# A decoder layer on one core: which engine splits the memory's weights, where the S5 output is split, who takes the heads' roots, and how the first norm is finished

## The chip, the core and the metric

The kernel runs on one core of a Trainium2 chip. The core has a matrix engine (TensorE, PE in the rows; its weight loads are shown as PEld), a vector engine (VectorE, DVE), a scalar engine (ScalarE, ACT), a general engine (POOL, GpSimd) and a queue for transfers (SyncE, SP). Each engine works through its own list in order; semaphores tie the lists together. The metric is the device time of one execution in microseconds, the median of several.

## The reference

One decoder layer in float32 for 1024 tokens of width 1024, with a memory of 256 tokens. Cut to what the change touches:

```
h = layer_norm(x); mem_n = layer_norm(mem)
z = h @ w_in                                   # S5 input | q k | v | r | low-rank gate
y_ssm = gelu-GLU of a diagonal state-space scan over 32 groups
o = chunked gated linear attention, 4 heads of 128 values
o = o * rsqrt(mean(o*o, -1) + 1e-5) * norm_g * silu(r)     # one root per token and head
y = concat(y_ssm, o) @ w_out
h = layer_norm(2**0.25 * h + y)                # the first norm of the layer
kv = mem_n @ w_mkv; p = softmax(q k^T / 16); h = layer_norm(2**0.25 * h + (p v) @ w_mo)
h = layer_norm(2**0.25 * h + relu(h @ w_ff1)**2 @ w_ff2)
```

## The kernel before

**Splits.** Products that need float32 accuracy are made of three products of rounded parts: `split` lets ScalarE write the rounded high part and VectorE or POOL subtract it from the source for the low part; `mm3` runs high x high, high x low, low x high. A weight block of 128 x 1024 elements (`weight`, `wcols`) is read into a `raw` buffer (four of them) through SP's queue and split into `hl`. Tables of bits (`MW`, `MW1`, `MV1` and the like) say block by block which engine subtracts: a one is VectorE, a zero POOL (`eng`). A bank of PSUM of 128 x 512 is taken by a letter: three `d`, three `s`, two `g`.

**Memory.** `mem_stream` folds the memory into two weights for each of four heads h: `a_d` (keys times w_mq) and `vw_d` (values times w_mo). For a head it transposes w_mq (`wqT`), multiplies the normed memory by the key columns (`mem_proj`, `mnT` x `hl`, result `kvT`), multiplies the two, loads the value columns, and multiplies those by w_mo. `mem_w` loads two key or two value blocks. Head 0 comes at the start of the program, heads 1 to 3 here.

**Filling.** A `Filler` holds streams of work cut into pieces of known cost and is told at fixed places in the program to run so many us of them. From the end of the S5 scan it alternates `glu_stream` (the GLU, which gates `Y0` by `y1f`, then `y_split`, which makes the parts of y that the output product reads, and the load of residual tiles `R`), and the rest of `mem_stream`; `out_stream` follows, the S5 half of the output product. Which instruction comes first on an engine is then set by a scheduler that sees the dependencies and its own costs, not by the text alone. `behind()` ties the instructions traced inside it, on VectorE alone, behind the last VectorE instruction traced before.

**Gated attention.** The chunk scores are built from seven levels. For each level and each half of the sequence (`level`), TensorE multiplies K and Q for two pairs of chunks into `g` banks (L1065), VectorE copies them by mask into `Am`, and then Q (VectorE one half of its rows, POOL the other) and K (POOL, mostly) are multiplied by the level's decay. The next level reads these. `diagonal` comes first: VectorE makes Q and the product `prod`, which lies in the tile `y1f`, and TensorE sums it against `ones2`. Then eight chunks (`gla_chunk`): update and state products, state S (POOL decays, VectorE adds), squares of the output per head by ScalarE with a sum, one root for each of 128 tokens and 4 heads (`rsqrt`, on `sq` of 128 x 4), and the scaling by ScalarE or VectorE (`ON`).

**First norm.** In the loop over `tk` the chunk `tk`, the parts of y for chunk `tk - 1` (`gla_out`) and the attention half of the output product for tile `tk - 2` (`block`, epilogue of `post_norm`) follow each other. The epilogue adds into `R`; after the second half the tile is normed by `layer_norm`, and three blocks later transposed into `h`, the operand of the next stage (L243, splits `h`). `norm_stats` takes the mean and the variance (`mv`) and a root of one column (`tq`, nine small VectorE instructions). Then, in columns:

- plain form: VectorE takes the mean off and multiplies by the gain over 1024 columns; ScalarE scales the upper 512 by the root; VectorE scales the lower 512 and adds the bias; POOL adds the bias to the upper 512;
- `light` form: VectorE does the first step on the lower 512 alone and makes the shift in one more small instruction, ScalarE norms the upper 512, and POOL multiplies and adds there, two instructions of 512 columns.

The bits of `GLN` = 53 choose light for tiles 0, 2, 4 and 5. The second norm (`ahead=True`) uses the same function and the same bits.

Of the kernel before, what the change touches and what calls it, by code (L numbers as in the profile page):

```python
# [17 lines left out]
P = 128  # L18
# [7 lines left out]
T = 8  # L26
# [18 lines left out]
MWU = 7  # L45
MQK = 3
MVV = 11
MW1 = 0
MV1 = 1
MO1 = 3  # L50
MQ0 = 255
ON = 206
# [29 lines left out]
def hybrid_layer(  # L82
# [61 lines left out]
    def stt(e, o, a, s, b, op0, op1):  # L144
        e.scalar_tensor_tensor(out=o, in0=a, scalar=s, in1=b, op0=op0, op1=op1)  # L145
# [16 lines left out]
        for n, (i, j) in enumerate(P3):  # L162
            PE.matmul(o, lhs(i), rhs(j), start=first and n == 0, stop=last and n == 2, skip_group_check=more)  # L163

    def rsqrt(e, y, v, t):
        ts(e, y.bitcast(I32), v.bitcast(I32), -0.5, 1597463007.0, ALU.mult, ALU.add)
        for _ in range(3):
            stt(e, t, y, -0.5, y, ALU.mult, ALU.mult)
            tt(e, t, t, v, ALU.mult)
            stt(e, y, t, 1.5, y, ALU.add, ALU.mult)  # L170

    def rsqrt1(y, v, eps, t):

        vh, w = t[:, 0:1], t[:, 1:2]
# [46 lines left out]
        rsqrt1(tq[:, 0:1], mv[:, 1:2], EPS, tq[:, 1:3])  # L221
        return mv, tq

    def layer_norm(xt, rows, light=False, st=None):
        mv, tq = norm_stats(xt, st)
        lo_, hi_ = slice(0, 512), slice(512, D)
        if light:
            stt(V, xt[:, lo_], xt[:, lo_], mv[:, 0:1], rows[:, 0, lo_], ALU.subtract, ALU.mult)
            stt(V, tq[:, 3:4], mv[:, 0:1], -1.0, tq[:, 0:1], ALU.mult, ALU.mult)
            act(xt[:, hi_], xt[:, hi_], AF.Identity, scale=tq[:, 0:1], bias=tq[:, 3:4])  # L230
            tt(G, xt[:, hi_], xt[:, hi_], rows[:, 0, hi_], ALU.mult)
        else:
            stt(V, xt, xt, mv[:, 0:1], rows[:, 0, :], ALU.subtract, ALU.mult)
            act(xt[:, hi_], xt[:, hi_], scale=tq[:, 0:1])
        stt(V, xt[:, lo_], xt[:, lo_], tq[:, 0:1], rows[:, 1, lo_], ALU.mult, ALU.add)
        tt(G, xt[:, hi_], xt[:, hi_], rows[:, 1, hi_], ALU.add)
# [750 lines left out]

    def y_split(th, k):
        hi, lo = (ya(0, th)[:, i, k, :].rearrange("p (c t) -> p c t", t=T) for i in range(2))
        split(hi, lo, Y0[:, k, :].rearrange("p (t c) -> p c t", t=T)[:, th * 64:(th + 1) * 64, :], scale=0.25)  # L990

    R = []

# [72 lines left out]


    prod = y1f[:, 0:2048].rearrange("p (a t) -> p a t", a=2)
    ones2 = const.tile([P, 2], F32, name="ones2")
    G.memset(ones2, 0.0)  # L1070
    for h in range(2):
        G.memset(ones2[hrow[h], h:h + 1], 1.0)

# [74 lines left out]
    def gla_chunk(tk):  # L1148
        ktm, on, sr, vt = K[:, :, tk * P:(tk + 1) * P], Am[:, tk].rearrange("p h t -> p (h t)"), sr_[tk % 2], v_[tk % 2]
        if tk < NT - 1:  # L1150
            up = bank("s", (P, 2, P))
            for a in range(2):
                for h in range(2):
                    PE.matmul(up[hrow[h], a, :], ktm[:, a, h * 64:h * 64 + 64],
                              vt[:, (2 * a + h) * P:(2 * a + h + 1) * P], start=True, stop=True)
        po = bank("g", (P, 4, P))
        for h in range(4):
            PE.matmul(po[:, h, :], Am[:, tk, h, :], vt[:, h * P:(h + 1) * P], start=True, stop=tk == 0)
            if tk:
                PE.matmul(po[:, h, :], Q[:, h // 2, h % 2, tk * P:(tk + 1) * P], S[:, h // 2, :], start=False, stop=True)  # L1160
        if tk < NT - 1:
            tt(G, S, S, dcl[:, :, tk:tk + 1].to_broadcast([P, 2, P]), ALU.mult)
            tt(V, S, S, up, ALU.add)
        if tk < NT - 2:
            gla_keys(tk + 1)
        sq = small.tile([P, 12], F32, tag="sq", name="sq")
        for h in range(4):
            act(on[:, h * P:(h + 1) * P], po[:, h, :], AF.Square, accum_out=sq[:, h:h + 1])
        ts(V, sq[:, 0:4], sq[:, 0:4], 1.0 / P, EPS, ALU.mult, ALU.add)
        rsqrt(V, sq[:, 4:8], sq[:, 0:4], sq[:, 8:12])  # L1170
        if ON >> tk & 1:
            for h in range(4):
                act(on[:, h * P:(h + 1) * P], po[:, h, :], scale=sq[:, 4 + h:5 + h])
        else:
            on4 = on.rearrange("p (h v) -> p h v", h=4)
            tt(V, on4, po, sq[:, 4:8].unsqueeze(2).to_broadcast([P, 4, P]), ALU.mult)
        tt(eng(OE, tk), on, on, sr, ALU.mult)
# [31 lines left out]
    def post_norm(put, rows, scale=ALPHA, ahead=False):  # L1209

        half = stage.tile([P, NT, 2, 6], F32, tag="cn", bufs=1, name="half") if ahead else None

        def epi(n, t, po):
            r = res(t)[:, n * 512:(n + 1) * 512]
            if scale is None:
                tt(V, r, r, po, ALU.add)
            else:
                stt(V, r, r, scale, po, ALU.mult, ALU.add)
            if n == 0:
                if ahead:  # L1220
                    V.bn_stats(out=half[:, t, 0, :], in_=r)
                late.append(lambda: None)
            else:
                layer_norm(res(t), rows, GLN >> t & 1, half[:, t] if ahead else None)
                late.append(lambda: put(t))
        return epi

# [482 lines left out]
```

## Time and profile before

| | us |
|---|---|
| median of 3 runs | 1414.79 (1411.76 to 1419.1) |
| the profiled execution | 1412.6 |
| its span | 1410.8 |
| TensorE busy | 1341.5 |
| VectorE busy | 998.0 |
| POOL busy | 460.0 |
| mean granted clock of TensorE | 0.986 |

How to read the rows: `325.10 4.63 PE L163 MATMUL ... x24 [2.22 <-DVE wqT L142]` in an order of time is the start, the length of the merged group, engine, line, operation, tile written <- tiles read, how many, and in brackets the idle time ahead of it on its engine with what ended that. L142 and L145 are the helpers `tt` and `stt`, L163 is the matmul of `mm3`, so groups are told apart by their tiles. The tile names `g` and `qk` stand for several slots: `g<-g,g` is a level's product on Q, `qk<-qk,g` that on K. Of the stages that follow: the S5 scan ends near 310, levels run from 318 to 457, chunks from 478 to 549, the first norm from 503 to 590.

### The profile page before, as it was taken

What the parts mean: (1) busy time and instruction counts of PE and PEld (TensorE: products, weight loads), DVE (VectorE), ACT (ScalarE), POOL (GpSimd) and SP (SyncE); (2) the same over time, 40 slices, a digit from 0 to 9 for tenths busy, and PEclk for the clock granted to TensorE, in tenths of its full rate; (3) what the DMA queues carried; (4) which work ended last, traced back from release to release, by engine and by line L of the source; (5) the groups of instructions that cost most, each with busy time, mean ns of one, the idle gap of its engine ahead of it and who ended that gap; (6) DMA issues with size and microseconds to landing.
All of it is one profiled execution on the core that took longest, in us unless ns stands there. A gap on an engine that the chain in (4) does not pass through costs nothing. (4 is left out here: it accounts for less than half of the span.)

```text
span 1410.8 us, 18927 instructions
## 1 busy us (share of the span) xinstructions
PE 1341.5 (95%) x6824; PEld 1112.6 (79%) x6824; DVE 998.0 (71%) x1783; ACT 570.1 (40%) x946; POOL 460.0 (33%) x338
## 2 busy tenths in 40 slices
PE   7798999999899998999998999999999999999997
PEld 6575788788898887788887777778888888888886
DVE  8999588756855489844478667766555676568797
ACT  4433532342545143333123654445545343335431
POOL 1663144312855133200014223443332142003364
PEclk9899999999999999999999999999999999999999
DMA  9722342543756120310120656554446985334432
GB/s 311 255 110 81 107 121 52 161 159 112 255 186 209 56 73 23 119 30 1 60 60 23 194 174 198 194 188 142 145 140 230 343 270 178 104 105 150 149 105 90
DMA packets 155513, 199.81 MB, mean 142 GB/s; under 512 B 16294, under 2 KB 86044, under 8 KB 155292
## 3 DMA queue, kind: packets, MB, share of 16 engines
q1 hardware_dynamic: 143536, 179.44, 39.5%
q10 hardware_dynamic: 11884, 19.17, 3.7%
q8 instruction: 54, 0.88, 0.3%
q14 instruction: 39, 0.32, 0.1%
HBM read 140.38 MB, written 58.20 MB: 141 GB/s over the span
## 5 line engine op out<-in xcount | busy, mean ns | idle before, releaser
L163 PE MATMUL ps_d<-xt,w1q 128*128 128x512 f32 x576 | 138.3, 391 | 9.8 <-DVE w1s L142 9.5
L163 PEld LDWEIGHTS ps_d<-xt,w1q 128*128 128x128 f32 x576 | 107.3, 188 | 35.4 <-issue 12.2
L142 POOL TENSOR_TENSOR hl<-raw,hl 128x1024 fp32r<-128x1024 f32 x21 | 63.0, 3006 | 168.3 <-ACT hl L148 168.2
L163 PE MATMUL ps_s<-cell 128*128 128x512 f32 x432 | 113.0, 389 | 0.0
L163 PE MATMUL ps_d<-cell 128*128 128x512 f32 x432 | 106.0, 389 | 0.4 <-DVE hid L142 0.4
L142 POOL TENSOR_TENSOR R<-R,row 128x512 f32<-128x512 f32 x42 | 57.8, 1386 | 138.4 <-ACT R L148 134.9
L163 PE MATMUL ps_d<-h0T,hl 128*128 128x512 f32 x384 | 93.6, 402 | 5.8 <-DVE hl L142 5.8
L163 PE MATMUL ps_g<-xb,w1q 128*128 128x512 f32 x384 | 94.3, 397 | 3.9 <-ACT hid L148 3.9
L163 PE MATMUL ps_d<-hl,y 128*128 128x512 f32 x384 | 95.1, 403 | 2.5 <-DVE y L142 2.5
L163 PEld LDWEIGHTS ps_d<-cell 128*128 128x128 f32 x432 | 81.0, 188 | 17.6 <-DVE hid L142 0.8
L163 PEld LDWEIGHTS ps_s<-cell 128*128 128x128 f32 x432 | 81.1, 188 | 16.8
L163 PEld LDWEIGHTS ps_d<-h0T,hl 128*128 128x128 f32 x384 | 73.2, 193 | 25.8 <-DVE hl L142 6.2
L163 PE MATMUL ps_d<-hl,h0T 128*128 128x512 f32 x384 | 91.1, 393 | 1.4 <-DVE h0T L142 1.3
L148 ACT ACTIVATE hl<-raw 128x1024 fp32r<-128x1024 f32 x62 | 64.8, 1059 | 66.1 <-PE ps_d L163 60.2
L163 PE MATMUL ps_d<-hl,p 128*128 128x512 f32 x384 | 89.0, 391 | 0.0
L163 PEld LDWEIGHTS ps_g<-xb,w1q 128*128 128x128 f32 x384 | 72.5, 191 | 19.6 <-ACT hid L148 4.7
L163 PEld LDWEIGHTS ps_d<-hl,y 128*128 128x128 f32 x384 | 72.6, 193 | 18.0 <-DVE y L142 3.0
L148 ACT ACTIVATE hid<-hid 128x512 f32<-128x512 f32 x112 | 70.8, 632 | 36.9 <-DVE hid L142 35.1
L163 PEld LDWEIGHTS ps_d<-hl,h0T 128*128 128x128 f32 x384 | 71.0, 188 | 17.3 <-DVE h0T L142 1.8
L163 PEld LDWEIGHTS ps_d<-hl,p 128*128 128x128 f32 x384 | 71.6, 188 | 14.6
L142 DVE TENSOR_TENSOR cell<-ha,cell 128x1024 fp32r<-128x1024 f32 x56 | 78.2, 1401 | 5.6 <-ACT cell L148 3.4
L148 ACT ACTIVATE w1q<-raw 128x512 fp32r<-128x512 f32 x80 | 50.0, 628 | 76.2 <-PE ps_d L163 39.6
(286 smaller groups left out, 2868.8 us busy)
## 6 DMA issues: line engine op xcount, KB each, us to landing
g_d<-hid SPq DMA_DIRECT2D x112, 256.0 KB
ha<-g_d SPq DMA_DIRECT2D x56, 512.0 KB
raw<-in_w_ff_dram SPq DMA_DIRECT2D x40, 512.0 KB
b<-in_w_ff_dram SPq DMA_DIRECT2D x32, 512.0 KB
raw<-in_w_mkv_dram SPq DMA_DIRECT2D x16, 512.0 KB
raw<-in_w_in_dram SPq DMA_DIRECT2D x16, 512.0 KB
wq<-in_w_mq_dram SPq DMA_DIRECT2D x8, 512.0 KB
xs<-in_x_dram SPq DMA_DIRECT2D x8, 512.0 KB
```

The costliest lines, as they stand in the source:

```text
L142: e.tensor_tensor(out=o, in0=a, in1=b, op=op)
L148: A.activation(out=o, in_=i, func=f, **kw)
L163: PE.matmul(o, lhs(i), rhs(j), start=first and n == 0, stop=last and n == 2, skip_group_check=more)
```

## The change

Four edits. `MW1` and `MV1` become 3: both key blocks and both value blocks of heads 1 to 3 are subtracted by VectorE (before, POOL did both key blocks and one of two value blocks; nine blocks move). `y_split` is traced inside `behind()`. In `gla_chunk` the root is no longer `rsqrt` (one instruction for the mean, one for the first guess, three rounds of three): ScalarE takes the square root of mean + 1e-5, VectorE its reciprocal and one Newton round. In the first norm no tile takes the light form any more, and tiles 5, 6 and 7 are finished by VectorE alone over 1024 columns, with neither ScalarE nor POOL.

```diff
-MW1 = 0
-MV1 = 1
+MW1 = 3
+MV1 = 3
...
-    def layer_norm(xt, rows, light=False, st=None):
+    def layer_norm(xt, rows, light=False, st=None, alone=False):
         mv, tq = norm_stats(xt, st)
         lo_, hi_ = slice(0, 512), slice(512, D)
+        if alone:
+            stt(V, xt, xt, mv[:, 0:1], rows[:, 0, :], ALU.subtract, ALU.mult)
+            stt(V, xt, xt, tq[:, 0:1], rows[:, 1, :], ALU.mult, ALU.add)
+            return
...
         hi, lo = (ya(0, th)[:, i, k, :].rearrange("p (c t) -> p c t", t=T) for i in range(2))
-        split(hi, lo, Y0[:, k, :].rearrange("p (t c) -> p c t", t=T)[:, th * 64:(th + 1) * 64, :], scale=0.25)
+        with behind():
+            split(hi, lo, Y0[:, k, :].rearrange("p (t c) -> p c t", t=T)[:, th * 64:(th + 1) * 64, :], scale=0.25)
...
-        ts(V, sq[:, 0:4], sq[:, 0:4], 1.0 / P, EPS, ALU.mult, ALU.add)
-        rsqrt(V, sq[:, 4:8], sq[:, 0:4], sq[:, 8:12])
+        rt_ = sq[:, 8:12]
+        act(rt_, sq[:, 0:4], AF.Sqrt, scale=1.0 / P, bias=eps_c)
+        V.reciprocal(sq[:, 4:8], rt_)
+        ts(V, sq[:, 0:4], sq[:, 0:4], -0.5 / P, -0.5 * EPS, ALU.mult, ALU.add)
+        tt(V, sq[:, 8:12], sq[:, 4:8], sq[:, 4:8], ALU.mult)
+        tt(V, sq[:, 8:12], sq[:, 8:12], sq[:, 0:4], ALU.mult)
+        stt(V, sq[:, 4:8], sq[:, 8:12], 1.5, sq[:, 4:8], ALU.add, ALU.mult)
...
-                layer_norm(res(t), rows, GLN >> t & 1, half[:, t] if ahead else None)
+                layer_norm(res(t), rows, ahead and GLN >> t & 1, half[:, t] if ahead else None, not ahead and t > 4)
```

(`eps_c` is a constant column of 1e-5; `rsqrt` is dropped.)

How the scheduler lays this out, at three places on VectorE. In these rows `g_2865` is Q, `g_2866` the score tile, `Y_2878` the GLU's tile, `y_...` the parts of y, `hl` a weight block. First, where the GLU's gating meets the first diagonal and head 1, before:

```order
L142 TENSOR_TENSOR glu_2880<-Y_2878,glu_2879 128x1024 x2
L142 TENSOR_TENSOR y1f<-qk 128x2x512
L142 TENSOR_TENSOR g_2865<-qk,g_2864 64x2x512
L145 SCALAR_TENSOR_TENSOR Y_2878<-y1f,Y_2878 128x512
L142 TENSOR_TENSOR g_2865<-qk,g_2864 64x2x512
L145 SCALAR_TENSOR_TENSOR Y_2878<-y1f,Y_2878 128x512
L142 TENSOR_TENSOR wqT<-ps_d,wqT 128x512 x2
```

and now:

```order
L142 TENSOR_TENSOR glu_2880<-Y_2878,glu_2879 128x1024 x2
L142 TENSOR_TENSOR hl<-raw,hl 128x1024 x2
L145 SCALAR_TENSOR_TENSOR Y_2878<-y1f,Y_2878 128x512
L142 TENSOR_TENSOR g_2865<-qk,g_2864 64x2x512
L145 SCALAR_TENSOR_TENSOR Y_2878<-y1f,Y_2878 128x512
L142 TENSOR_TENSOR g_2865<-qk,g_2864 64x2x512
L142 TENSOR_TENSOR y1f<-qk 128x2x512
L142 TENSOR_TENSOR wqT<-ps_d,wqT 128x512 x2
```

Two key blocks of head 1, formerly POOL's, stand ahead of the gating, and the diagonal's product has moved behind the two products on Q; wqT keeps its place behind them all. On TensorE the sums of that product moved with it, from ahead of the transposes of w_mq to ahead of the memory product.

Second, the second half of the first level (from its mask copies on) and what lies up to the second level, before:

```order
L142 TENSOR_TENSOR hl<-raw,hl 128x1024
L145 SCALAR_TENSOR_TENSOR y_3254<-Y_2878,y_3254 128x512
L1110 COPY_PREDICATED g_2866<-mask,ps_g 128x512 x2
L142 TENSOR_TENSOR g_2865<-g_2865,g_2864 64x2x256
L145 SCALAR_TENSOR_TENSOR y_3254<-Y_2878,y_3254 128x512
L145 SCALAR_TENSOR_TENSOR y_3385<-Y_2878,y_3385 128x512 x4
L142 TENSOR_TENSOR kvT<-ps_d,kvT 128x512
L1110 COPY_PREDICATED g_2866<-mask,ps_g 128x256x2 x2
```

and now:

```order
L142 TENSOR_TENSOR hl<-raw,hl 128x1024
L145 SCALAR_TENSOR_TENSOR y_3255<-Y_2878,y_3255 128x512
L1110 COPY_PREDICATED g_2866<-mask,ps_g 128x512 x2
L142 TENSOR_TENSOR g_2865<-g_2865,g_2864 64x2x256
L145 SCALAR_TENSOR_TENSOR y_3255<-Y_2878,y_3255 128x512
L142 TENSOR_TENSOR hl<-raw,hl 128x1024 x2
L142 TENSOR_TENSOR kvT<-ps_d,kvT 128x512
L1110 COPY_PREDICATED g_2866<-mask,ps_g 128x256x2 x2
L142 TENSOR_TENSOR g_2865<-g_2865,g_2864 64x2x128x2
L145 SCALAR_TENSOR_TENSOR y_3255<-Y_2878,y_3255 128x512
L145 SCALAR_TENSOR_TENSOR y_3386<-Y_2878,y_3386 128x512 x3
```

Four of the splits that stood ahead of kvT have moved behind the second level's mask copies; two key blocks of head 2 stand ahead of kvT in their place.

Third, the norm of tile 5 from the last split of y on, before:

```order
L142 TENSOR_TENSOR y_4879<-ps_s,y_4879 128x4x128
L145 SCALAR_TENSOR_TENSOR tq<-tq 128x1
L145 SCALAR_TENSOR_TENSOR tq<-mv,tq 128x1
L145 SCALAR_TENSOR_TENSOR R_4108<-R_4108,tq,row 128x512
L142 TENSOR_TENSOR R_4108<-R_4108,ps_d 128x512
L142 TENSOR_TENSOR wa<-raw,wa 128x1024
```

and now:

```order
L142 TENSOR_TENSOR y_4846<-ps_s,y_4846 128x4x128
L145 SCALAR_TENSOR_TENSOR tq<-tq 128x1
L142 TENSOR_TENSOR wa<-raw,wa 128x1024
L145 SCALAR_TENSOR_TENSOR tq<-tq 128x1
L142 TENSOR_TENSOR R_4109<-R_4109,ps_d 128x512
L145 SCALAR_TENSOR_TENSOR R_4109<-R_4109,tq,row 128x1024
```

The last step of the norm, now over 1024 columns, stands behind the subtraction for the next stage's weight block `wa`, where it stood ahead of it.

More of the change, by code (lines that the diff above doesn't have):

```diff
@@ L163, in mm3 @@
             PE.matmul(o, lhs(i), rhs(j), start=first and n == 0, stop=last and n == 2, skip_group_check=more)
[L165 to L170, printed above, removed]
     def rsqrt1(y, v, eps, t):
@@ L1068, in hybrid_layer @@
     prod = y1f[:, 0:2048].rearrange("p (a t) -> p a t", a=2)
-    ones2 = const.tile([P, 2], F32, name="ones2")
+    ones2 = const.tile([P, 4], F32, name="ones2")
+    ones2, eps_c = ones2[:, 0:2], ones2[:, 2:3]
     G.memset(ones2, 0.0)
+    G.memset(eps_c, EPS)
     for h in range(2):
```

## The prediction

> **What bounds the kernel now.** First the page's head and engines, then the table of stretches (PE, PEld, DVE, ACT and POOL busy, granted clock, DMA).
>
> ```profile
> span 1410.8 us, 18927 instructions
> PE 1341.5 (95%) x6824; PEld 1112.6 (79%) x6824; DVE 998.0 (71%) x1783; ACT 570.1 (40%) x946; POOL 460.0 (33%) x338
> ...
> 315.00:346.00 31.00, 28.24 (x167) 24.73 (x166) 20.52 (x21) 7.74 (x12) 12.14 (x5) 0.94 0.40 133
> 346.00:376.00 30.00, 25.32 (x170) 23.18 (x169) 26.89 (x23) 17.72 (x21) 22.44 (x7) 0.94 0.55 184
> 376.00:480.00 104.00, 104.00 (x714) 94.32 (x713) 53.11 (x63) 39.59 (x63) 47.47 (x29) 1.00 0.56 183
> 504.00:565.00 61.00, 55.88 (x333) 46.64 (x332) 58.02 (x171) 24.00 (x82) 20.93 (x18) 0.97 0.11 32
> 565.00:575.00 10.00, 7.05 (x30) 5.75 (x29) 9.97 (x16) 4.29 (x6) 5.44 (x3) 0.83 0.41 119
> ```
>
> TensorE works 95% of the span, so only its gaps can be won. Of the stages that the change touches four have gaps: 2.76 us from 315 to 346, 4.68 from 346 to 376, 5.12 from 504 to 565, 2.95 from 565 to 575, in all 15.5. In the last three VectorE is 90 to 100% busy: there it is the bound. From 376 to 480 TensorE has no gap, and VectorE is half idle. Next, TensorE's order of time with what ended each gap, one line of the waits view (total, times, longest), and one stretch for its clock.
>
> ```profile
> 325.10 4.63 PE L163 MATMUL ps_d<-mnT,hl 128*128 128x256 f32 x24 [2.22 <-DVE wqT L142]
> 333.66 3.04 PE L163 MATMUL ps_d<-mnT,hl 128*128 128x256 f32 x24
> 359.73 6.00 PE L163 MATMUL ps_d<-mnT,hl 128*128 128x256 f32 x48
> 369.11 3.15 PE L1065 MATMUL ps_g<-g,qk 128*128 128x128 f32 x16 [3.38 <-DVE g L142]
> 374.41 3.90 PE L163 MATMUL ps_d<-hl,kvT 128*128 128x512 f32 x16 [1.30 <-DVE kvT L142]
> 378.15 1.98 PE L1065 MATMUL ps_g<-g,qk 128*128 128x128 f32 x16
> 521.09 2.98 PE L163 MATMUL ps_d<-hl,y 128*128 128x512 f32 x12
> 557.41 4.14 PE L163 MATMUL ps_d<-hl,y 128*128 128x512 f32 x10 [2.52 <-DVE y L142]
> 571.71 1.11 PE L243 MATMUL ps_s<-ident,R 128*128 128x128 f32 x4 [2.95 <-POOL R L142]
> 572.48 3.99 PE L163 MATMUL ps_d<-hl,y 128*128 128x512 f32 x12
> ...
> PE ps_s L1154 <- DVE h L142: 2.6, 2, 1.3
> ...
> 325.00:330.00 5.00, 4.90 (x29) 4.90 (x29) 4.82 (x6) 0.00 (x0) 0.00 (x0) 0.66 0.57 185
> ```
>
> A gap of over 2.2 us costs twice: 24 matmuls take 4.63 us behind the gap of 2.22 and 3.04 elsewhere, at a granted clock of 0.66. The like stands behind 3.38 (3.15 us for what takes 1.98), 2.52 (4.14 for ten where twelve take 2.98) and 2.95 (3.99 for 2.98, and slow transposes). That is about 1.6 us four times, 6.3 in all. Behind 1.30 nothing is slow: sixteen matmuls take 3.90, four thirds of 2.98. So 15.5 + 6.3 = 21.8 us are at stake.
>
> Why VectorE is late shows where its order of time is laid beside POOL's (with one line of the groups).
>
> ```profile
> 313.97 3.49 POOL L142 TENSOR_TENSOR hl<-raw,hl 128x1024 fp32r<-128x1024 f32 x1 [21.53 <-ACT hl L148]
> 315.12 3.42 DVE L142 TENSOR_TENSOR y1f<-qk 128x1024 f32<-128x1024 f32 x1
> 319.40 2.52 POOL L142 TENSOR_TENSOR hl<-raw,hl 128x1024 fp32r<-128x1024 f32 x1
> 319.60 2.87 DVE L145 SCALAR_TENSOR_TENSOR Y<-y1f,Y 128x512 f32<-128x512 f32 x1
> 328.64 1.22 DVE L142 TENSOR_TENSOR y1f<-qk 128x1024 f32<-128x1024 f32 x1
> 342.60 1.23 DVE L142 TENSOR_TENSOR hl<-raw,hl 128x1024 fp32r<-128x1024 f32 x1
> 361.12 2.50 DVE L142 TENSOR_TENSOR hl<-raw,hl 128x1024 fp32r<-128x1024 f32 x1
> 364.97 10.99 POOL L142 TENSOR_TENSOR hl<-raw,hl 128x1024 fp32r<-128x1024 f32 x2
> 366.00 2.45 DVE L1110 COPY_PREDICATED g<-mask,ps_g 128x512 f32<-128x512 uint8 x2
> 368.89 4.86 DVE L145 SCALAR_TENSOR_TENSOR y<-Y,y 128x512 fp32r<-128x512 f32 x5
> 373.68 0.67 DVE L142 TENSOR_TENSOR kvT<-ps_d,kvT 128x512 fp32r<-128x512 f32 x1
> ...
> L142 POOL TENSOR_TENSOR qk<-qk,g 128x512 f32<-128x512 f32 x13 | 20.7, 1595 | 1.0
> ```
>
> The two engines take turns. VectorE's product at 315.12 lasts until POOL's subtraction ends at 317.46 and 1.1 us on; alone the same product takes 1.22. The one at 319.60 ends 0.55 after POOL's at 321.92. Five y splits in a row, 368.89 to 373.75, hold POOL off in turn: its two subtractions take 10.99 us. Reads of PSUM (mask copies, kvT) show no such wait.
>
> **The change part by part.** I replay by hand: the rows of the new order, each starting when its engine and its releaser are done, with the durations above and 0.97 for a y split.
>
> *Weights (MW1, MV1).* Nine subtractions of 128x1024 go from POOL, 2.5 us each when unhindered, to VectorE: 1.23 alone, 2.50 behind a turn of POOL, so 11 to 22 us more for VectorE. Five fall before 376, four between 376 and 445. First gap: two of them now stand ahead of the gated products at 315.12, but POOL subtracts nothing there, and clears Q early. 315.1 + 2.4 (two subtractions) + 1.2 (two Y) + 2.4 (two g) + 1.2 (y1f) = 322.3 for y1f, and 323.5 with the two wqT behind it; TensorE used to start the memory product at 325.10. In the new order nearly all `ones` products, which read y1f, stand ahead of it and fill the time until wqT. TensorE comes to them at about 321.8 (325.10 less the gaps of 2.22 and 0.54 and the four `ones` products that stood there), so some 0.5 us of waiting is left, at full clock: **3.9 us** come back of the 4.4 at stake (2.76 and 1.6). Bounds 0, if the two subtractions are hindered, and 4.4.
>
> *y splits (`behind`).* Their eight subtractions stay, each behind the last VectorE instruction traced. Second gap, in times shifted by 3.9: VectorE now does mask copy, subtraction, mask copy, Q product, subtraction, Y, split, subtraction, split, two mask copies, Q product. From 347.8 that is 2.5 + 0.8 + 3 x 1.2 + 0.7 + 2 x 1.0 + 2.5 + 0.7 = 12.8 without turns; two pairs of POOL's level products (3.2 us a pair) stand against it, and I count 1.8 of them: 362.4. TensorE arrives at 365.7 - 3.9 = 361.8, so 0.7 is left of 3.38. Then one split and two subtractions stand before kvT, 3.5 us, where five splits took 4.86: 1.1 is left of 1.30. Neither is long enough to slow the clock: **4.4 us** of 6.3 (4.68 and 1.6). The five later splits lie behind mask copies, and the first reader of y is the output product after 445. Bounds 0 (hindered subtractions undo the pin) and 6.3.
>
> *Roots by ScalarE, and the first norm.* One line of the tile view (least, median, longest), then the chunks' rows in order of time:
>
> ```profile
> L145 DVE SCALAR_TENSOR_TENSOR sq<-sq x48: 140/161/1268, 481.9 to 557.5; 128x4 f32<-128x4 f32 x48
> ...
> 527.33 0.68 DVE L142 TENSOR_TENSOR R<-R,ps_d 128x512 f32<-128x512 f32 x1
> 533.03 2.65 POOL L142 TENSOR_TENSOR R<-R,row 128x512 f32<-128x512 f32 x2 [3.95 <-ACT R L148]
> 533.35 1.00 DVE L145 SCALAR_TENSOR_TENSOR sq<-sq 128x4 f32<-128x4 f32 x1
> 539.91 1.35 DVE L145 SCALAR_TENSOR_TENSOR R<-R,mv,row 128x1024 f32<-128x1024 f32 x1
> 564.63 2.40 POOL L142 TENSOR_TENSOR wa<-raw,wa 128x1024 fp32r<-128x1024 f32 x1 [4.41 <-ACT wa L148]
> 565.04 2.00 DVE L145 SCALAR_TENSOR_TENSOR tq<-tq 128x1 f32<-128x1 f32 x1
> ...
> 142.10 1.28 ACT L148 ACT_TABLE_LOAD   x1
> 548.90 0.32 ACT L148 ACTIVATE g<-ps_g 128x128 f32<-128x128 f32 x1
> ```
>
> Eleven small instructions a chunk become five, 48 fewer: 7.7 us by the median of 0.16, less where they overlap wide neighbours. Those that meet POOL's turn count more: 1.00 while POOL adds its halves at 533.03, 2.00 while it splits wa. Tiles 0, 2 and 4 now have one POOL half instead of two, 5 to 7 none. The price: the first product of tiles 0, 2, 4 and 5 and the last of 5, 6 and 7 grow from 512 to 1024 columns, half of 1.35 each, 4.7 us on VectorE. ScalarE's root of 128x4 is shown nowhere; it lies between 0 and the 0.32 of a 128x128, and I take 0.3, the nearest row. The reciprocal that waits for it has behind it, on VectorE, the norm's chain, the residual additions and the h and y splits for which TensorE waits; but in the order it stands behind the state's addition, which waits for POOL after the chunk's last matmul, about as long as ScalarE squares. So it adds nothing; with that cover gone 0.3 a chunk, 2.4. Two table loads of 1.28: one in chunk 0, where VectorE has idle time, one before the first softmax, whose transposes come two blocks later. Nothing; uncovered 2.6.
>
> VectorE was 3.3 us behind TensorE at 527.33 (the block ended at 524.07). In the replay it is 1.9 behind there and 1 a chunk later: both waits for h go, **2.6 us** (bounds 0.6 and 2.6). The y split of chunk 6 ends near 552.8, with TensorE there at 552.3 (557.41 - 2.52 - 2.6): 0.5 is left, **3.6 us** of 2.52 + 1.6 (bounds 0 and 4.1). At 571.71 POOL's halves of tile 5 go, and VectorE's wide last product takes their place, behind wa's subtraction, which still takes its turn after POOL's wa. TensorE gets there 26 matmuls after the last y transposes; the product ends 1.3 to 2.0 later, with the slow clock or without: **2.0 us** of 4.5 (bounds -2 and 4.5).
>
> Here a page can be weighed: the Trainium skill, TensorE: Matmul & The Clock Gate, What's actually happening, has the clock fall after about one idle window of 3.4 us. The trace disagrees, the clock is 0.66 behind 2.22 us. By the page the remainder of tile 5 is free of the slow clock, and the sum 1 us larger.
>
> Four subtractions between 376 and 445 may push a mask copy: 0 to 4.9 us, I take 1, as VectorE is half idle. On SP's queue two blocks of w_mo pass three residual tiles, all early. Sum: 3.9 + 4.4 + 2.6 + 3.6 + 2.0 - 1.0 = **15.5 us**. The profiled execution took 1412.6 (span 1410.8), so 1397.1; the median of the runs lies 2.2 above it: 1399.3. A replay by hand leaves out what lies between an event and its waiter, so I say **1400.5**.
>
> **The rivals.** *A swap.* VectorE pays for its own subtractions what it gains from POOL's missing turns: 2.2 + 2.3 at 315 and 319, some 1 to 2 later, about 6 us, and five subtractions cost 6.2. Then the second gap stays, and only half of the first (2) and the two waits for h (2.6) are won, about 5: 1410. For it: VectorE's 26.89 of 30 us. Against: the order puts four splits behind kvT. The Trainium skill, Perfetto Trace Analysis, Optimizing Scalar/DVE Operations, warns that moving work between these two engines might not help, since they share a port; the turns in the rows agree.
>
> *VectorE, already the bound, is given more (slower).* From 315 to 376 five subtractions at the hindered 2.50 are 12.5 us, from 504 on the wide products 4.7, less 4 x 0.97 for splits moved behind kvT, and nothing from roots that overlap: 13.3 us, 1428. It decides if subtractions and level products alternate throughout. Against: POOL's 22.44 us from 346 to 376 lose the 10.99 and one more, to about 9.
>
> *All gaps go.* 21.8 us: 1393. Against: tile 5 stays behind wa.
>
> **How the numbers follow.** Forecast 0.62, swap 0.19, slower 0.10, all gaps gone 0.09. The forecast's own range, with its two largest unknowns (the second gap and tile 5) at either bound, is 1394 to 1407. With the swap and the edge of the largest case it is 1393 to 1411.5; the slower case stays out. Within 0.5%, 7 us, is about what a measurement here can't tell from no change: faster 0.70, same 0.20, slower 0.10.
>
> **What would show it.** Right: no wait of over 1 us for wqT near 323; y1f and Y at 1.2 and 0.7; under 1 us before the second level's products near 362; no gaps at the L1154 products; VectorE's additions under 2 us behind their blocks; a wait of 1 to 2 us for R, by VectorE, near 555; no new gap from 376 to 480; nothing but a shift later. Wrong: subtractions of 2.5 us before kvT and over 3 us of gap there, reciprocals that wait for ScalarE, or over 3 us for R.

## The result, and the profile after

The changed kernel took 1401.5 us (median of six runs, 1398.6 to 1403.2), the kernel before 1415.6 on the same chip (six runs, 1411.8 to 1420.5): a ratio of 0.989, 95% interval 0.987 to 0.991. Predicted were 1400.5 us, with a range of 1393 to 1411.5, and faster as the likeliest outcome. The profiled execution is the slowest of the six (1403.2 us), while the one profiled before (1412.6 us) lies near the lower end of the times before. First the head of its page.

```profile
span 1401.4 us, 18861 instructions
PE 1340.5 (96%) x6824; PEld 1111.5 (79%) x6824; DVE 988.6 (71%) x1740; ACT 573.7 (41%) x953; POOL 419.5 (30%) x323
```

The span is therefore only 9.4 us shorter, where the medians differ by 14.1. To see where, I cut both traces at six marks that TensorE passes in both programs: the first glu product, the second memory product of 24 matmuls, the third `wq` transposes, the first transposes of keys (L1145), the first `wa` product, and the first softmax transposes. These are their rows in the changed kernel's order of time.

```profile
318.21 5.95 PE L163 MATMUL ps_d<-glu,hl 128*128 128x512 f32 x24
335.93 3.04 PE L163 MATMUL ps_d<-mnT,hl 128*128 128x256 f32 x24
381.86 1.04 PE L362 MATMUL ps_d<-ident,wq 128*128 128x128 f32 x8
478.33 0.38 PE L1145 MATMUL ps_s<-ident,qk 128*128 128x128 f32 x2
566.71 2.88 PE L163 MATMUL ps_d<-wa,h 128*128 128x512 f32 x12
590.33 0.60 PE L1273 MATMUL ps_s<-ident,prob 128*128 128x128 f32 x4
```

Before, the same marks lie at 312.12, 333.66, 381.35, 477.84, 576.30 and 599.90. The changed kernel reaches the first mark 6.1 us later (in code that the change doesn't touch; more on that below) and the last 9.6 us earlier. So between the marks it wins 15.7 us: 287.78 become 272.12. By stretch, with letters for the terms of the prediction's sum: A is its first gap (3.9), B the second (4.4), C the two waits for h (2.6), D the wait for y (3.6), E the wait for R of tile 5 (2.0), F the subtractions between 376 and 445 (-1.0).

| stretch | before | changed | won | predicted |
|---|---|---|---|---|
| 1: glu product to second memory product (A) | 21.54 | 17.72 | 3.8 | 3.9 |
| 2: to the third wq transposes (B) | 47.69 | 45.93 | 1.8 | 4.4 |
| 3: to the first key transposes (F) | 96.49 | 96.47 | 0 | -1.0 |
| 4: to the first wa product (C, D, E) | 98.46 | 88.38 | 10.1 | 8.2 |
| 5: to the softmax transposes | 23.60 | 23.62 | 0 | 0 |

Stretch 1 went by the replay. TensorE's and then VectorE's order of time, in the changed kernel:

```profile
328.44 1.72 PE L1082 MATMUL ps_g<-ones,y1f 128*128 128x2 f32 x14 [0.47 <-DVE y1f L142]
330.02 3.12 PE L163 MATMUL ps_d<-mnT,hl 128*128 128x256 f32 x24
...
321.20 2.36 DVE L142 TENSOR_TENSOR hl<-raw,hl 128x1024 fp32r<-128x1024 f32 x2
327.15 1.23 DVE L142 TENSOR_TENSOR y1f<-qk 128x1024 f32<-128x1024 f32 x1
```

The two subtractions took 2.36 together, y1f 1.23 instead of 3.42, and 0.47 of waiting is left, where 0.5 was said. Stretch 2 did not go by it. TensorE there, then VectorE and POOL:

```profile
368.05 2.06 PE L1063 MATMUL ps_g<-g,qk 128*128 128x128 f32 x16
370.92 0.73 PE L163 MATMUL ps_d<-hl,kvT 128*128 128x512 f32 x2 [0.81 <-ACT kvT L148]
373.29 5.54 PE L163 MATMUL ps_d<-hl,kvT 128*128 128x512 f32 x16 [1.64 <-DVE kvT L142]
...
368.81 1.20 DVE L142 TENSOR_TENSOR hl<-raw,hl 128x1024 fp32r<-128x1024 f32 x1
370.42 2.22 DVE L142 TENSOR_TENSOR hl<-raw,hl 128x1024 fp32r<-128x1024 f32 x1 [0.40 <-ACT hl L148]
372.56 0.68 DVE L142 TENSOR_TENSOR kvT<-ps_d,kvT 128x512 fp32r<-128x512 f32 x1
...
370.26 1.30 POOL L142 TENSOR_TENSOR g<-g,g 64x512 f32<-64x512 f32 x1 [2.90 <-PE ps_g L1063]
```

The second level comes with no wait at all (3.38 before). But kvT, behind it, now costs 0.81 + 1.64 of waiting, and the 16 matmuls behind take 5.54 instead of 3.90: the slow clock is back. What stands ahead of kvT on VectorE is two subtractions of weights for the next head. The first took 1.20; the second started 0.40 late, behind ScalarE's copy, and took 2.22, since POOL's level product had begun at 370.26, just ahead of it.

Stretch 4, TensorE:

```profile
524.48 0.66 PE L1154 MATMUL ps_s<-qk 128*64 128x128 f32 x8
534.07 0.66 PE L1154 MATMUL ps_s<-qk 128*64 128x128 f32 x8
549.12 5.74 PE L163 MATMUL ps_d<-hl,y 128*128 128x512 f32 x24
563.49 1.06 PE L240 MATMUL ps_s<-ident,R 128*128 128x128 f32 x8 [1.41 <-DVE R L145]
564.31 2.57 PE L163 MATMUL ps_d<-hl,y 128*128 128x512 f32 x10
```

Both waits for h are gone, that for y (2.52) too, and R's is 1.41 instead of 2.95, ended by VectorE, with ten matmuls at full clock behind it. All three terms are as good as predicted, or better. ScalarE's two added table loads (at 481.91 and 576.39, 1.28 each) made TensorE wait nowhere, and stretch 5 is unchanged, as predicted.

### The profile page after: what moved, and what is told of

Read it like the earlier page. It is cut to its first block, busy times and chain, and to the rows that moved or that the text cites. A ratio compares the mean times of both kernels' runs of the same rounds, so it can differ in the third digit from the quotient of the medians.

```text
span 1401.4 us, 18861 instructions
## 1 busy us (share of the span) xinstructions
PE 1340.5 (96%) x6824; PEld 1111.5 (79%) x6824; DVE 988.6 (71%) x1740; ACT 573.7 (41%) x953; POOL 419.5 (30%) x323
## 5 line engine op out<-in xcount | busy, mean ns | idle before, releaser
L163 PE MATMUL ps_d<-hl,y 128*128 128x512 f32 x384 | 92.2, 394 | 0.0
L142 POOL TENSOR_TENSOR R<-R,row 128x512 f32<-128x512 f32 x35 | 47.6, 1369 | 118.2 <-ACT R L148 115.1
L142 DVE TENSOR_TENSOR hl<-raw,hl 128x1024 fp32r<-128x1024 f32 x50 | 66.4, 1336 | 21.3 <-ACT hl L148 20.9
```

Of the source, the lines that this page charges most:

```text
L142: e.tensor_tensor(out=o, in0=a, in1=b, op=op)
```

## The experiments

The question is which part won what, why the second gap gave so little, and whether the 6.1 us ahead of the first mark belong to the change. My theory is the prediction's: VectorE's order and its turns with POOL set TensorE's gaps. The rivals are the swap (what VectorE gains from POOL's missing turns it pays for its own subtractions), the simple sum of independent parts, and chance. This table gives the stretches of every profile (us, cut at the marks above), and the times (median; ratio to the kernel before in runs on the same chip, with its interval).

| kernel | 1 | 2 | 3 | 4 | time | ratio |
|---|---|---|---|---|---|---|
| before | 21.54 | 47.69 | 96.49 | 98.46 | | 1 |
| changed | 17.72 | 45.93 | 96.47 | 88.38 | 1401.5 | 0.989 (0.987 to 0.991) |
| weights alone | 17.72 | 49.62 | 96.93 | 99.82 | 1415.1 | 0.999 (0.998 to 1.001) |
| pin alone | 20.07 | 42.65 | 96.48 | 96.23 | 1409.8 | 0.995 (0.993 to 0.998) |
| roots alone | 20.05 | 47.59 | 96.51 | 91.77 | 1408.3 | 0.993 (0.991 to 0.996) |
| first norm alone | 20.08 | 47.60 | 96.50 | 93.08 | 1409.8 | 0.995 (0.993 to 0.998) |
| changed, once more | 19.23 | 45.91 | 96.47 | 88.35 | 1400.4 | 0.987 (0.985 to 0.988) |
| keys behind kvT | 19.22 | 42.63 | 98.24 | 88.38 | 1400.9 | 0.988 (0.985 to 0.990) |
| keys and copies behind | 17.72 | 41.34 | 96.83 | 88.36 | 1395.1 | 0.983 (0.982 to 0.985) |
| head 1's keys only | 19.25 | 42.87 | 96.49 | 88.38 | 1399.2 | 0.986 (0.984 to 0.988) |
| changed without weights | 20.04 | 42.68 | 96.50 | 88.36 | 1400.6 | 0.990 (0.987 to 0.992) |
| keys and copies, again | 17.71 | 41.34 | 96.80 | 88.35 | 1397.5 | 0.986 (0.984 to 0.989) |
| the same, wa by VectorE | 19.25 | 41.33 | 96.81 | 86.81 | 1396.1 | 0.986 (0.983 to 0.988) |

The four single parts ran on one chip, the next four on one, and the last three on one; the kernel before took 1415.7, 1419.6 and 1417.3 there, so times are compared within a chip only.

### The weights edit alone

```diff
-MW1 = 0
-MV1 = 1
+MW1 = 3
+MV1 = 3
```

> The kernel before with the weights edit alone (MW1 = 3, MV1 = 3). My theory (VectorE's order, and its turns with POOL, set TensorE's gaps): the first product y1f takes 1.2 us instead of 3.42, the gap before wqT falls from 2.22 to under 1 and 3.8 us are won there, as in the changed kernel. But the y splits are not pinned, so the two subtractions for head 2 stand on VectorE behind five splits and ahead of kvT, with two mask copies and a level product: kvT comes some 5 us later than before, and the second gap takes back what the first gave. Sum within 2 us of no change. The swap: VectorE pays for its own subtractions what it gains; nothing is won at wqT, and the sum is 3 to 5 us slower. Additive parts: this edit alone is worth its 3.9 us, and the second gap stays at 3.4 + 1.3.

TensorE in the second stretch, and the rows of VectorE that it waits for:

```profile
362.93 2.05 PE L1065 MATMUL ps_g<-g,qk 128*128 128x128 f32 x16 [1.08 <-DVE g L142]
371.17 2.90 PE L1065 MATMUL ps_g<-g,qk 128*128 128x128 f32 x12 [5.24 <-DVE g L1110]
...
363.70 1.20 DVE L142 TENSOR_TENSOR hl<-raw,hl 128x1024 fp32r<-128x1024 f32 x1
364.83 3.87 DVE L145 SCALAR_TENSOR_TENSOR y<-Y,y 128x512 fp32r<-128x512 f32 x4
368.63 1.21 DVE L142 TENSOR_TENSOR hl<-raw,hl 128x1024 fp32r<-128x1024 f32 x1
369.76 2.41 DVE L1110 COPY_PREDICATED g<-mask,ps_g 128x512 f32<-128x512 uint8 x2
```

The first gap was won as in the changed kernel (17.72). The level's wait fell from 3.38 to 1.08, but then five splits (the first at 362.71, not shown), two subtractions and two mask copies run in a row: one wait of 5.24. It is ended by the mask copies, which TensorE needs first, and not by kvT as I had expected. Stretch 2 is 1.9 us longer than before, the ratio 0.999. The sum came out as my theory had it; what the swap expected (nothing won at wqT) and what independent parts expected (3.9 us) did not.

### The pinned y splits alone

```diff
-        split(hi, lo, Y0[:, k, :]..., scale=0.25)
+        with behind():
+            split(hi, lo, Y0[:, k, :]..., scale=0.25)
```

> The kernel before with the pinned y splits alone. My theory: one split less ahead of the second level (it took 2.33 us behind POOL), one instead of five ahead of kvT, so the gap of 3.38 falls to about 1, that of 1.30 goes, and with it the slow clock (1.6): 4 to 5 us faster, without the weights edit. The swap: POOL's two subtractions, no longer held off by the five splits, hold up VectorE's level products and kvT instead; gaps stay at over 2.2 in sum with the slow clock, at most 2 us are won. Nothing changes at wqT (2.22) or from 504 on in either.

```profile
330.10 3.14 PE L163 MATMUL ps_d<-mnT,hl 128*128 128x256 f32 x24 [2.22 <-DVE wqT L142]
369.86 2.06 PE L1066 MATMUL ps_g<-g,qk 128*128 128x128 f32 x16 [0.62 <-DVE g L142]
372.15 4.64 PE L163 MATMUL ps_d<-hl,kvT 128*128 128x512 f32 x18 [0.23 <-ACT kvT L148]
555.88 2.57 PE L163 MATMUL ps_d<-hl,y 128*128 128x512 f32 x10 [2.50 <-DVE y L142]
```

Waits of 0.62 and 0.23 are left of 3.38 and 1.30, and stretch 2 falls by 5.0 us. The pin does alone what I had given to it together with the weights edit, and more than both do together (1.8). The swap's "at most 2" is wrong here. Two rows hold a surprise: behind the wait of 2.22 for wqT the 24 matmuls take 3.14, at full clock, and behind that of 2.50 for y ten take 2.57. In the profile before, 4.63 and 4.14 stood behind waits of 2.22 and 2.52. The last section comes back to this.

### The heads' roots by ScalarE alone

```diff
-        ts(V, sq[:, 0:4], sq[:, 0:4], 1.0 / P, EPS, ALU.mult, ALU.add)
-        rsqrt(V, sq[:, 4:8], sq[:, 0:4], sq[:, 8:12])
+        rt_ = sq[:, 8:12]
+        act(rt_, sq[:, 0:4], AF.Sqrt, scale=1.0 / P, bias=eps_c)
+        V.reciprocal(sq[:, 4:8], rt_)
+        ...
```

> The kernel before with the heads' roots by ScalarE alone. My theory: six small instructions a chunk less, 1 us of VectorE a chunk by the median; both waits for h (2.6) go and the y split's gap (2.52 + 1.6) shrinks to 0.5 to 1.5: 4 to 6 us faster; the gap before R at tile 5 (2.95, ended by POOL) stays, since POOL's halves stay. Rival (the reciprocal waits for ScalarE's root, with the norm's chain queued behind it): idle time of VectorE of 0.3 us or more before the reciprocals, and at most 2 us won. Rival (it is POOL's halves, not VectorE's small instructions, that make h late): the waits for h stay.

TensorE, and ScalarE's roots in the view of the tile `sq` (least, median, longest in ns):

```profile
532.02 0.66 PE L1156 MATMUL ps_s<-qk 128*64 128x128 f32 x8 [0.17 <-DVE h L142]
563.29 1.12 PE L243 MATMUL ps_s<-ident,R 128*128 128x128 f32 x4 [2.94 <-POOL R L142]
...
L148 ACT ACTIVATE sq<-sq,ones x8: 297/298/299, 480.9 to 544.5; 128x4 f32<-128x4 f32 x8
```

Stretch 4 is 6.7 us shorter, a little more than the 4 to 6 I expected: the waits for h fall from 2.60 to 0.17 and that for y goes. R's wait stays at 2.94, ended by POOL. So with VectorE's small instructions gone h and y come in time although POOL's halves stay, which the second rival had excluded. The next kernel shows the other side of it: with fewer halves, and all the small instructions, h comes in time too. And the reciprocal's wait for ScalarE cost nothing that shows: the root takes 0.30.

### The first norm alone

```diff
...
-                layer_norm(res(t), rows, GLN >> t & 1, half[:, t] if ahead else None)
+                layer_norm(res(t), rows, ahead and GLN >> t & 1, half[:, t] if ahead else None, not ahead and t > 4)
```

> The kernel before with the edit of the first norm alone. My theory: the gap before R at tile 5 falls from 2.95 to between 1 and 2.5 and is ended by VectorE, its slow clock goes with it (1 to 2 us won there); the waits for h and the y split shrink by about 1 us in all, since tiles 0, 2 and 4 have one POOL half less to take turns with, but the small instructions of the roots remain: 2 to 3 us faster. The swap: the wide products cost VectorE 4.7 us on the bound of this stage, the waits for h and y grow by what R gains, and the sum is within 1 us of no change.

```profile
550.32 2.60 PE L163 MATMUL ps_d<-hl,y 128*128 128x512 f32 x10 [0.52 <-DVE y L142]
559.81 2.57 PE L163 MATMUL ps_d<-hl,y 128*128 128x512 f32 x10 [1.16 <-DVE y L142]
568.49 3.04 PE L163 MATMUL ps_d<-hl,y 128*128 128x512 f32 x12 [1.58 <-DVE y L142]
571.71 1.06 PE L247 MATMUL ps_s<-ident,R 128*128 128x128 f32 x8 [0.18 <-DVE R L145]
```

(The form `alone` in `layer_norm` is as in the change.) 5.4 us won in stretch 4, where I expected 2 to 3. The waits for h are down to 0.21 and R's to 0.18; VectorE's lateness now shows earlier, at y, in three waits of which the longest is 1.58, and one of 0.67 for g is ended by POOL. All are at full clock. Before, y and R took 2.52 and 2.95, both with slow matmuls behind them. The swap, which had at most 1 us for this part, is out. Roots and norm win 6.7 and 5.4 alone and 10.1 together: they share the waits for h.

### What held up kvT: the next head's keys behind it

```diff
-                nxt = mem_load(h + 1)
+                with behind(): nxt = mem_load(h + 1)
```

This pins only VectorE's subtractions of the next head's key weights. A second kernel pins ScalarE's copies of them behind its copy of kvT as well:

```diff
-                with behind(): nxt = mem_load(h + 1)
+                with behind(), tc.issue_after(last_of(A)): nxt = mem_load(h + 1)
```

where `last_of(A)` stands for the last ScalarE instruction traced, found as `behind` finds VectorE's.

> The changed kernel with one more pin: the subtractions of the next head's key weights queue behind kvT on VectorE. The pin alone won 5.0 us between the second memory product and the third wq transposes (47.69 to 42.65 us), and with the weights edit the changed kernel keeps only 1.8 of it (45.93). My theory: the loss is the two subtractions for head 2 (1.20 and 2.22 us) ahead of kvT, and the slow clock (1.6) behind the 0.81 and 1.64 of waiting. With them behind kvT the stretch takes 42.6 to 43.3: ScalarE's copy of kvT still stands behind that of the weights, so some 0.8 of waiting stays, at full clock. 2.5 to 3.5 us faster than the changed kernel, about 17 faster than before. Rival (the level products' turn with POOL is what holds kvT up): the wait for kvT stays above 1.5 and the stretch above 44.5.

> As the run before it, and ScalarE's copies of these weights queue behind its copy of kvT as well. My theory: the last 0.8 before kvT shrinks to 0.3, the stretch takes 42.0 to 42.6, and no new wait appears up to 480, since TensorE is not short of weights there: 3 to 4 us faster than the changed kernel, ratio to the kernel before about 0.987. Rival (the weights of head 2 then come too late): a gap before the key product of head 2 behind 381, and nothing won over the changed kernel.

TensorE's wait in the first:

```profile
369.19 4.66 PE L163 MATMUL ps_d<-hl,kvT 128*128 128x512 f32 x18 [0.77 <-ACT kvT L148]
411.47 3.14 PE L163 MATMUL ps_d<-mnT,hl 128*128 128x256 f32 x24 [1.58 <-ACT vst L148]
```

And in the second, with VectorE's kvT:

```profile
367.46 4.37 PE L163 MATMUL ps_d<-hl,kvT 128*128 128x512 f32 x18
366.59 0.69 DVE L142 TENSOR_TENSOR kvT<-ps_d,kvT 128x512 fp32r<-128x512 f32 x1
```

The subtractions were the cause: with them behind kvT, stretch 2 takes 42.63 and one wait of 0.77 is left, by ScalarE, as expected; with the copies behind as well it takes 41.34 with no wait, less than the 42.0 I expected, and VectorE's kvT comes at 366.59. The first kernel shows no gain in its time (1400.9 against 1400.4 for the changed kernel on that chip, where I expected 2.5 to 3.5 us). Its profile has a wait of 1.58 at 411.47 that no other has, for a copy that itself waited for a write to DRAM, and the slow clock in stretch 1; its four runs spread from 1399.4 to 1406.1. So its time decides nothing. The second is faster than the changed kernel with no overlap: 1394.2 to 1397.4 against 1399.0 to 1401.9. It beats both kernels.

### Only head 1's keys on VectorE

```diff
-        bits = {0: MW, D: MV0}.get(c0, MV1 if c0 >= D else MW1)
+        bits = {0: MW, D: MV0, 256: 3}.get(c0, MV1 if c0 >= D else MW1)
```

with MW1 = 0 and MV1 = 1 as before.

> The changed kernel with the weights edit cut down to the two key blocks of head 1; POOL keeps the seven other subtractions. My theory (the two key blocks of head 1 hold the whole gain of the weights edit, the others only cost): 17.7 us from the glu product to the second memory product as in the changed kernel, and 42.3 to 43.5 from there to the third wq transposes as with the pin alone: 2.5 to 3.5 us faster than the changed kernel, ratio about 0.987. Rival (turns: POOL's subtractions between 350 and 376 hold up VectorE's level products again): a gap of over 2 before the second level or kvT, and the stretch above 44.5, no faster than the changed kernel.

```profile
368.62 4.66 PE L163 MATMUL ps_d<-hl,kvT 128*128 128x512 f32 x18 [0.47 <-ACT kvT L148]
```

Two of the nine moved subtractions hold all that the weights edit wins in TensorE's waits. With the other seven back on POOL, stretch 2 takes 42.87, as with the pin alone, and no gap in it is over 0.6. Stretch 1 shows the same wait for y1f as in the changed kernel (0.45) and again the slow clock behind it. The time, 1399.2, is not told apart from the changed kernel's 1400.4 (five runs from 1395.1 to 1403.0); the 2.5 to 3.5 us that I expected are not shown.

### The whole change without the weights edit

```diff
-MW1 = 3
-MV1 = 3
+MW1 = 0
+MV1 = 1
```

> The changed kernel without the weights edit (MW1 = 0, MV1 = 1 as before; pin, roots and norm stay). By the stretches measured so far the weights edit wins 2.3 us (3.8 where the clock is slow behind wqT) up to the second memory product and loses 3.3 from there to the third wq transposes on top of the pin, so without it: 20.1 or 21.5 us for the first stretch (the wait of 2.22 for wqT is back), 42.6 for the second, 96.5 and 88.4 for the others: the same time as the changed kernel within 2 us. My reading (the weights edit as a whole is worth nothing in this change): within 0.2% of the changed kernel's 0.987 to 0.989. Rival (it carries its 3.9 us as predicted, and kvT's wait has another cause): about 4 us slower than the changed kernel, 0.990 to 0.992, and kvT's wait of over 2 us still there.

```profile
328.09 3.12 PE L163 MATMUL ps_d<-mnT,hl 128*128 128x256 f32 x24 [2.22 <-DVE wqT L142]
370.14 4.66 PE L163 MATMUL ps_d<-hl,kvT 128*128 128x512 f32 x18 [0.23 <-ACT kvT L148]
```

The pin, the roots and the norm stay. The wait of 2.22 is back, kvT's is 0.23, and from the first mark to the softmax transposes it takes 271.1 us, where the two profiles of the changed kernel have 272.1 and 273.5. The ratio, 0.990, has an interval that overlaps both of the changed kernel's, which itself did not run on this chip. Within what these runs can tell, the weights edit as a whole is worth nothing in this change: it wins at wqT and gives it back at kvT.

### The faster version again, and R's last wait

> The kernel with the next head's key weights behind kvT on VectorE and ScalarE, once more, for the comparison on one chip with the two others of this call: 4 to 5 us faster than the changed kernel (its stretch 41.3 instead of 45.9), ratio to before 0.983 to 0.986. Rival (its 0.983 was a lucky draw of the varying transfers and clock): 0.987 to 0.989.

> That kernel with POOL's share of wa given to VectorE as well (MD = 251, which also moves one block of the later dense product with the same numbering). In the changed kernel TensorE waits 1.41 us for R of tile 5; on VectorE the step of the root took 1.77 us instead of 0.15, until POOL's subtraction of wa ended. My theory: with POOL's gone the step takes 0.15, VectorE reaches R's last product 1.6 us earlier, and the wait falls from 1.41 to under 0.3: 1.1 to 1.4 us faster than without it, visible in the profile and hardly in the times. Rival (a swap: the added subtraction of 1.2 on VectorE comes ahead of what TensorE needs next): a new wait of about 1 at the first products of wa or at the next R, and nothing won up to the softmax.

```diff
-MD = 250
+MD = 251
```

This comes on top of the pinned keys and copies.

In the changed kernel VectorE had this step of the root, behind POOL's subtraction of wa:

```profile
558.58 1.77 DVE L145 SCALAR_TENSOR_TENSOR tq<-tq 128x1 f32<-128x1 f32 x1
...
557.93 2.40 POOL L142 TENSOR_TENSOR wa<-raw,wa 128x1024 fp32r<-128x1024 f32 x1 [6.21 <-ACT wa L148]
```

With POOL's gone (VectorE, then TensorE):

```profile
553.62 0.21 DVE L145 SCALAR_TENSOR_TENSOR tq<-tq 128x1 f32<-128x1 f32 x1
...
556.97 1.06 PE L240 MATMUL ps_s<-ident,R 128*128 128x128 f32 x8
```

The step takes 0.21, R's wait of 1.41 is gone, and stretch 4 is 1.5 us shorter (86.81), with no new wait. In the times this can't be seen: 1396.1 against 1397.5. The version with keys and copies pinned was again ahead of a kernel with the changed one's time (1394.9 to 1398.5 against 1399.8 to 1403.4 without the weights edit, on the same chip); its ratio, 0.986, lies where the two expectations meet. On the one chip its median is 3.1 us lower, where 4 to 5 were expected against the changed kernel.

### The changed kernel once more

> The changed kernel once more, unaltered. In its profile the S5 scan waited 1.96 us for a transfer of taps and the glu product started at 318.21; before it was 0.50 and 312.12, in code that the change doesn't touch. In four kernels with one part each it was 0.58, 1.53, 0.56 and 1.67. My theory (it varies from execution to execution of the same program): 0.5 to 2 us of waiting, on either side, and where it is about 0.5, the glu product at 312 and a span of some 1396. Rival (the change shifts it): 1.5 to 2 again and 317 to 318. Ratio to before 0.989 in both.

VectorE's wait for the transfer of taps in the S5 scan, in the first profile of the changed kernel:

```profile
210.31 3.32 DVE L142 TENSOR_TENSOR s<-par 128x288 f32<-128x288 f32 x4 [1.96 <-DMA taps_d<-s]
```

And in the second, with stretch 1 on TensorE:

```profile
209.09 3.32 DVE L142 TENSOR_TENSOR s<-par 128x288 f32<-128x288 f32 x4 [0.56 <-DMA taps_d<-s]
327.74 4.61 PE L163 MATMUL ps_d<-mnT,hl 128*128 128x256 f32 x24
372.50 5.53 PE L163 MATMUL ps_d<-hl,kvT 128*128 128x512 f32 x16 [1.65 <-DVE kvT L142]
```

The same program waited 1.96 us for taps once and 0.56 the other time, and reached the first mark at 318.21 and 315.93. Over all thirteen profiles the mark lies between 311.89 and 318.21, and among the four single-part kernels, at 312.06, 317.11, 311.89 and 317.67. Ahead of the mark all thirteen traces have the same instructions in the same order on TensorE, VectorE and ScalarE, and the same transfers; on POOL the kernels with the new roots have one memset more, at 0.9 us. So the kernels with the pin or the norm alone, at 317, run nothing there that the kernel before does not, and the 6.1 us are at least in part a difference between executions. My expectation that a wait of about 0.5 goes with 312 did not hold, though: a second wait in the scan, of 1.91 at 253.29, stayed. What does go with the mark is TensorE's clock in the scan: the three profiles at 312 are the three whose granted clock never fell between 200 us and the mark; in the ten others it fell once or twice. Whether the whole change shifts the mark by a microsecond or two on the mean is open (the eight profiles that hold most of it all lie from 314.20 up). The wait for kvT and its slow clock, on the other hand, came back to within 0.01.

## Why the prediction was right, and where it was wrong

**The time is right, and the sum is right by terms that make up for one another.** 15.5 us were predicted, 15.7 and 14.3 found between the marks in the two profiles. B gave 2.6 less than said, F 1.0 more, C to E 1.9 more. That these cancel is luck. The forecast's own range is also not quite what its bounds give: from 1399.3, with the second gap and tile 5 at either bound, they give 1395 to 1408 and not 1394 to 1407. It changes nothing here.

**A, first gap: right in the wait, unsure in the clock.** The replay said 0.5 of waiting, measured 0.47. But the 1.6 us of slow clock that were part of the 3.9 are not reliably there to win, and that they came out in the first pair of profiles is luck. With the old order there were five profiles, and only the first has slow matmuls behind the 2.22. With the new order there were eight, and four have them, behind a wait of only 0.45 and the fourteen two-column products that follow it. Between the four full-clock profiles of the old order (20.04 to 20.08) and the four of the new (17.71 and 17.72) lie 2.3 us.

**B, second gap: the step that failed.** The working said: "Then one split and two subtractions stand before kvT, 3.5 us, where five splits took 4.86: 1.1 is left of 1.30", and "Neither is long enough to slow the clock". The three took 1.05, 1.20 and 2.22, and the second subtraction waited 0.40 for ScalarE's copy of its weights: 4.87 in all, no less than the five splits. I had priced both subtractions as unhindered and counted POOL's level products against VectorE only ahead of the second level; the second subtraction met the turn of the next one. And as the level's wait went away entirely, TensorE stood at kvT that much sooner. It waited 0.81 + 1.64 = 2.45 where the working left 0.7 + 1.1, and the matmuls behind took 5.54 instead of 3.90: 0.65 and 1.6 of the missing 2.6, so the slow clock is the larger share. The sign named for being wrong (subtractions of 2.5, over 3 of gap) was nearly there. The runs show it from both sides: without the weights edit kvT waits 0.23, with the two subtractions behind it 0.77 or nothing. The pin, alone, is worth 5.0 us, and the moved weights take 3.3 back. My forecast put down to both parts what one wins and the other loses. The swap was right for this edit in its result (nothing won in sum), wrong on where: not at wqT, which it gave half, but at kvT, through weights whose first product comes ten microseconds later (372.64, where the second subtraction ends, to 382.71 in the changed kernel's order of time).

Here the page that I weighed against the change holds for that edit: the Trainium skill, Perfetto Trace Analysis, Optimizing Scalar/DVE Operations, warns that moving work between VectorE and POOL might not help, and the kernel without the nine moved subtractions is as fast as the one with them. The first gap alone (17.72 against 20.05, at full clock) speaks for the move.

**C and D: right.** Both waits for h and that for y are gone. The cost of ScalarE's root, taken as 0.3 from a wider row, was 0.30; VectorE's one wait for a root in the changed kernel is 0.3. The roots do all of this alone; the norm alone does C too, but not D.

**E: right in kind.** 1.3 to 2.0 of waiting were said, behind POOL's turn for wa, and 1.41 was there; taking POOL's subtraction away removed it. The clock stayed full, so 3 us came back instead of 2.0.

**F: nothing.** Four more subtractions in stretch 3 cost nothing (96.47 against 96.49): VectorE was half idle there, and the 1.0 was a guess between its bounds.

**What gaps cost in clock.** I took 1.6 us for each gap over 2.2 as fixed. As the last section shows, it depends on where the gap falls in the windows of the clock. At the waits of 2.22 and 2.52, half of the 6.3 us, it went both ways; behind the six waits of 2.94 to 3.38 it was there each time. The range held it.

## What to carry to other kernels

When work is moved to an engine that others wait for, look not only at what the moved instructions cost but at what they stand ahead of: here two early, unneeded subtractions cost as much as the two useful ones won, and an issue-order pin behind the needed one gave 4.6 us in its stretch, about 0.3% of the time. Price such an instruction by its hindered duration (here 2.22 instead of 1.20) whenever the other engine has an operation of the kind that hindered it, here POOL's level product, ready at about that moment. And test parts of a change alone and left out: four parts that look additive here were one that wins and loses, one that wins alone, and two that share a gain.

## What the runs showed of the hardware

**The slow clock comes in windows of 3.41 us, and whether a gap brings it depends on where it falls in them.** Matmuls behind the same wait of 2.22 us for wqT took 4.63 us in one profile and about 3.1 in four others with the same order; behind 2.50 to 2.52 for y, ten took 4.14 and 4.06 in two and 2.57 in a third. At 2.94 and 2.95 all three were slow, and at 3.27 to 3.38 all three; at 1.16 to 1.69 in stretches 3 and 4 none was. And a short wait can do it if little work stands beside it: 0.45 us ahead of fourteen products of two columns (1.72 us in all) was followed by slow matmuls in four of eight profiles, among them one of two of the same program (3.12 and 4.61 for the 24 behind it); 0.81 and 1.64 with only two matmuls between, in both.

The clock as the traces record it explains this. In all thirteen the granted clock is 1.0 or 0.5, and it changes only on a grid of 3.41 us, which keeps its phase through an execution and has another in the next; a spell of half clock lasts one or more whole windows of that grid (but for the one at the end of the program). Here are two such windows around the wait of 2.22, from the kernel before and then from the pin alone (window and length; busy time of PE, PEld, DVE, ACT and POOL; granted clock; DMA).

```profile
322.02:325.44 3.42, 1.20 (x6) 0.72 (x5) 3.36 (x5) 0.69 (x1) 1.65 (x1) 1.00 0.68 228
325.44:328.85 3.41, 3.41 (x18) 3.41 (x17) 3.37 (x5) 0.00 (x0) 0.00 (x0) 0.50 0.71 232
...
326.26:329.68 3.42, 1.61 (x8) 1.00 (x6) 3.36 (x4) 0.69 (x1) 2.40 (x2) 1.00 0.48 156
329.68:333.09 3.41, 2.99 (x25) 2.99 (x26) 3.37 (x5) 0.00 (x0) 0.00 (x0) 1.00 0.89 303
```

In the first the wait lies within one window, TensorE is busy for 1.20 us of it, and the next window has half the clock. In the second the wait reaches into the next window, TensorE is busy for 1.61, and the clock stays. Between the first mark and the last, the thirteen traces have 1027 windows at full clock. In 16 of them TensorE was busy for at most 1.39 us, the two-column products not counted, and each of the 16 was followed by half clock; in all others it was busy for at least 1.56, and none was. So what counts is how much TensorE does in a window, and equal gaps end differently because the grid lies differently in each execution. The limit between 1.39 and 1.56 is read off these stretches: in the scan ahead of them, with its many short products, windows with 1.7 to 2.1 us of busy time were followed by half clock too.

The Trainium skill, TensorE: Matmul & The Clock Gate, What's actually happening, says that the activity window runs freely, without regard to the program, and gives it about 3.4 us; the grid in these traces agrees with both. Its table has the clock fall after an idle window. That the traces do not bear out: 1.20 us of work in the window above did not hold the clock.

**The wait for one transfer of the same program was 1.96 us or 0.56**, as the taps' rows show. Together with the clock this moved more than some of the edits did: in the two profiles of the changed kernel the first mark differs by 2.3 us and stretch 1 by 1.5.
